# Tiles of x sums and mixer weights 64 bytes later, one product moved up, two splits and the first loads in another order

## The chip, the cores and the metric

The kernel runs on one core of one Trainium2 chip. The metric is the device time of one execution in microseconds. The profile gives names to the engines: PE (TensorE: matmuls; PEld is its weight load), DVE (VectorE), ACT (ScalarE), POOL (GpSimd) and SP (SyncE, which issues most of the DMAs).

## The reference

One decoder layer on x of 512 tokens by 1024 features, float32:

```python
x = x + 0.5 * rms_norm(swiglu_ffn(rms_norm(x, norm_pre[0]), ffn1_w_in, ffn1_w_out), norm_post[0])
mixed = token_mixer(rms_norm(x, norm_pre[1]), w_mix_in, conv_w, conv_b, gate_bias, lb, hg_norm, ml_norm, w_mix_out)
x = x + rms_norm(mixed, norm_post[1])
x = x + 0.5 * rms_norm(swiglu_ffn(rms_norm(x, norm_pre[2]), ffn2_w_in, ffn2_w_out), norm_post[2])

def swiglu_ffn(x, w_in, w_out):
    gate, up = jnp.split(x @ w_in, 2, axis=-1)      # 1024 -> 2 x 2816
    return (jax.nn.silu(gate) * up) @ w_out         # 2816 -> 1024
```

The token mixer projects h with one matrix, runs two chunked recurrences (HGRN2 and mLSTM, four heads each) and projects back.

## The kernel before

**Three products for one.** The big matmuls run in the type float32r. An operand is cast into a "hi" part by ACT, and DVE takes the rest (operand minus hi) into a "lo" part; both lie in one tile, hi first. A product is then hi·hi + hi·lo + lo·hi, three matmuls. For a weight tile this is a *split* (`split`, L195 the cast on ACT, L197 the subtraction on DVE, 128x1024 each). Behind its split an item may add one raw tile into another on POOL (L209), for the products that follow.

**The first matmul of an FFN** takes fewer products by block sums of x and of the weights. The 11 column pairs t = 0..10 each need seven products p1..p7 (pair 0 is done in parts named c1..c4 and e1..e4). One product is 24 matmuls of 128x128 by 128x256 (`prod`, L456): the stationary operand is a weight tile `w`, the moving one is a tile of x. The left operands: p1, p2, p4 and p5 read the tiles `xq`, p3, p6 and p7 read the tiles `sq`, which hold sums of x. So four of seven products of a pair move `xq`, three move `sq`. A constant list gives the order; for the first pairs it is written out, and from the fifth pair on a pair t has p1 of t, p4 of t-1, then p3, p5, p7, p6, p2 of t.

```python
ORDER = HEADS + [(p, 1) for p in ("p7", "p5", "p3", "p6")] + [("p5", 2), ("p7", 2), ("p3", 2), ("p4", 1), ("p6", 2)]
```

Pair index 2 is called the third pair here, index 3 the fourth. `feed` splits weights ahead in that order, into four `w` tiles; raw weights come in by DMA from SP. After a product `after` combines the PSUM banks on DVE and ACT (L475 to L489). After p6 these are n, q and the new half of the hidden tile (`hf<-q,ps`), in that order on DVE; the last one reads the bank of p7, into which p4 of the same pair accumulates. So p4 of a pair waits for the step behind p6 of that pair.

**Where the tiles lie.** The kernel's allocation before puts the four `xq` at byte 33440 + 8192 n of each partition, the four `w` at 87008 + 8192 n and the three tiles of the ring "s" at 179936 + 8192 n. The ring "s" holds first `sq` and then, in the second matmul of the FFN, the split hidden tiles `hs`. Modulo 128, `xq` begin at 32, `w` and the ring "s" at 96. Rows inside a tile are multiples of 512 bytes apart.

**The second matmul of an FFN** has `hs` stationary and `w` moving, 512 columns (`mm3`, L125 to L127). **The mixer** has jobs of two kinds: `in_k` (L409) with `w` stationary and `xq` moving, 256 columns, and `t_mm` (by `mm3`, L125 to L127) with `xq` stationary and `w` moving, 512 columns; the output projection is of the second kind. These have weight tiles of 2 by 512.

**The begin.** SP and ACT issue the loads of x by rows of 128 (i) and halves (h); the norm's gain row comes as one row and is spread over the partitions by PE (`gain_pe`, L114). `spin` issues matmuls of the identity whose result is not used (L121). Then rows 0 and 1 are normed (L329 to L348), turned by PE (L244) and split (L264, L266), and the product c1 begins.

**The head of the second FFN** (`ffn_head`) does the same for x of that stage while the output projection of the mixer ends. `behind(i)` makes what is traced in it come later on its engine than the instruction i. Outside the begin, a scheduler places each engine's instructions, by what it takes to be ready.

Of the kernel before, what the change touches and what calls it, by code (L numbers as in the profile page):

```python
# [19 lines left out]
ND = D // P  # L20
NF = FF // P
EPS = 1e-6
RAW, WBUF = 3, 4
PAIRS = NF // 2
HALF = T // 2
KH = ND // 2
# [13 lines left out]
HEAD = 3  # L40
HEADS = [("c1", 0), ("c3", 0), ("c2", 0), ("c4", 0), ("p1", 1), ("e1", 0), ("e3", 0)]
HEADS += [("e2", 0), ("p1", 2), ("p2", 1), ("e4", 0), ("p2", 2)]
ORDER = HEADS + [(p, 1) for p in ("p7", "p5", "p3", "p6")] + [("p5", 2), ("p7", 2), ("p3", 2), ("p4", 1), ("p6", 2)]
for _t in range(HEAD, PAIRS):
    if _t == HEAD:
        ORDER += [("p1", _t), ("p3", _t), ("p5", _t), ("p4", _t - 1)] + [(p, _t) for p in ("p7", "p6", "p2")]
    else:
        ORDER += [("p1", _t), ("p4", _t - 1)] + [(p, _t) for p in ("p3", "p5", "p7", "p6", "p2")]

# [9 lines left out]
class Item:  # L59

    def __init__(self, key, loads, rows=None, adds=(), dst=None):
        self.key, self.loads, self.rows, self.adds, self.dst = key, loads, rows, adds, dst
        self.reads = {key, *(k for pair in adds for k in pair)}


class Layer:
# [32 lines left out]
    def gain_pe(self, tag, row):  # L101

        nc = self.nc
        g = self.cp.tile([P, D], F32, tag=tag, bufs=1, name=self.nm(tag))
        r = self.hf[0:1, 14:16, :].rearrange("p a t -> p (a t)")
        nc.sync.dma_start(r, row)
        one = self.st("one", P)[:1]
        nc.gpsimd.memset(one, 1.0)
        self.spare = self.ps()
        self.spin(3)  # L110
        for h in range(2):
            ps = self.ps()
            v = slice(512 * h, 512 * h + 512)
            nc.tensor.matmul(ps, one, r[:, v], start=True, stop=True)  # L114
            nc.vector.tensor_copy(g[:, v], ps)
        return g
# [67 lines left out]
    def split(self):  # L184

        nc = self.nc
        it = self.items.popleft()
        raw = self.raw[it.key]
        _, a, b = raw.shape
        w = it.dst() if it.dst else self.wp.tile([P, 2, a, b], F32R, tag="w", bufs=WBUF, name=self.nm("w"))  # L190
        hi, lo = w[:, 0], w[:, 1]
        self.ready.append((w, it.dst is not None))
        rows = it.rows
        if rows is None:
            nc.scalar.copy(hi, raw)  # L195
            yield
            nc.vector.tensor_tensor(lo, raw, hi.bitcast(F32), op=ALU.subtract)  # L197
        else:
            for j in range(a):
                nc.scalar.activation(hi[:, j], raw[:, j], AF.Copy, scale=rows[:, j : j + 1])  # L200
            yield
            for j in range(a):
                nc.vector.scalar_tensor_tensor(
                    lo[:, j], raw[:, j], rows[:, j : j + 1], hi[:, j].bitcast(F32), op0=ALU.mult, op1=ALU.subtract
                )
        with self.behind(*self.hold):
            for out, other in it.adds:
                o, c = self.raw[out], self.raw[other]
                nc.gpsimd.tensor_tensor(o, o, c, op=ALU.add)  # L209
        self.load_due(self.done)  # L210
        self.done += 1
        yield

    def feed(self, most=WBUF):

# [55 lines left out]
    def sums(self, i, src):  # L271


        nc = self.nc
        v = slice((i % 2) * P, (i % 2 + 1) * P)
        f = [x[:, :, v] for x in self.xf]
        sub = lambda out, a, b: nc.vector.tensor_tensor(out, a, b, op=ALU.subtract)  # L277
        hi = lambda dst, src: nc.scalar.copy(dst[:, 0, :, v], src)
        lo = lambda dst, src: sub(dst[:, 1, :, v], src, dst[:, 0, :, v].bitcast(F32))
        p1, p0 = self.turn(src, 1), self.turn(src, 0)  # L280
        a22 = self.hf[:, 10 + i, :].rearrange("p (c t) -> p c t", c=KH)
        s1, s2, s3, s4 = self.xq[2], self.sq[2], self.sq[1], self.sq[0]
        hi(self.xq[2], p0)
        hi(self.xq[3], p1)
        nc.scalar.copy(a22, p1)
        lo(self.xq[2], p0)
        lo(self.xq[3], p1)
        yield
        sub(p1, p0, a22)
        sub(p0, f[0], p0)  # L290
        hi(s3, p0)
        lo(s3, p0)
        yield
        sub(p0, f[0], p1)
        hi(s1, p1)
        lo(s1, p1)
        yield
        hi(s2, p0)
        sub(p1, f[1], p0)
        lo(s2, p0)  # L300
        yield
        hi(s4, p1)
        lo(s4, p1)
        yield
# [127 lines left out]
    def open_ffn(self, ctx):  # L432

        hp = self.hpool = ctx.enter_context(self.tc.tile_pool(name=self.nm("hp"), bufs=1))
        self.hf = hp.tile([P, NF, T], F32, name=self.nm("hf"))
        self.xf = [self.hf[:, j : j + 2, :].rearrange("p a (b t) -> p (a b) t", t=HALF) for j in (NF - 4, NF - 2)]
        self.sq = [hp.tile([P, 2, KH, HALF], F32R, tag="s", bufs=3, name=self.nm("sq")) for _ in range(3)]
        self.left = {"p1": self.xq[0], "p2": self.xq[1], "p4": self.xq[3], "p5": self.xq[2], "p6": self.sq[2], "p7": self.sq[1], "p3": self.sq[0]}
        self.left.update({"c1": self.xq[0], "c2": self.xq[1], "c3": self.xq[0], "c4": self.xq[1]})
        self.left.update({"e1": self.xq[2], "e2": self.xq[3], "e3": self.xq[2], "e4": self.xq[3]})  # L440
        self.gs, self.held, self.copies = [], {}, []
        self.hs, self.bank, self.later, self.n, self.q, self.had = deque(), {}, deque(), {}, {}, set()
# [68 lines left out]
    def ffn_head(self, trans):  # L511

        norm, seen = self.normed, self.col()
        norm.append(self.nc.gpsimd.tensor_copy(seen, self.hf[:, 17, T - 1 :]))
        self.hold = norm[2:]
        self.full_split()
        with self.behind(*self.added):
            for _ in range(2):  # L520
                self.full_split()
        with self.behind(*norm):
            for g in self.copies:
                next(g)
            self.feed()
        S = lambda: [next(g) for g in self.gs]
        then = {("e1", 0): S, ("e3", 0): S, ("e2", 0): S, ("e4", 0): S}
        for n, (p, t) in enumerate(HEADS):
            self.feed()
            self.lag()  # L530
            self.prod(p, t)
            self.after(p, t)
            if n == 0:
                with self.behind(*norm):
                    trans(2)
            elif n == 2:
                trans(3)
            elif (p, t) in then:
                then[p, t]()
        self.hold = ()  # L540
        self.holes()

    def start(self, norm, xn):
# [2 lines left out]
        norm(1)  # L546
        q = [[self.part(i, h, xn[i]) for h in range(2)] for i in range(2)]
        step = lambda *gs: [next(g) for g in gs]
        self.spin(4)
        step(q[0][0], q[0][1], q[0][0])  # L550
        self.spin(4)
        split = self.split()
        step(q[1][0], q[1][1])
        next(split)
# [72 lines left out]

    def h_tile(self, k2, dst=None):

        t = dst if dst is not None else self.hpool.tile([P, 2, 2, T], F32R, tag="s", bufs=3, name=self.nm("hs"))  # L630
        src = self.hf[:, 2 * k2 : 2 * k2 + 2, :]
        self.nc.scalar.copy(t[:, 0], src)
        self.nc.vector.tensor_tensor(t[:, 1], src, t[:, 0].bitcast(F32), op=ALU.subtract)  # L633
        return t
# [106 lines left out]
    def mix_items(self):  # L741
# [2 lines left out]

        def item(src, a, b, rows=None):
            key = ("mix", len(made))
            made.append(Item(key, [Load(key, src, a, b)], rows))

        def f(c0):
            for n in range(4):  # L750
# [14 lines left out]
    def ffn_items(self, name, w_in, w_out):  # L765
# [26 lines left out]
        for p, t in ORDER:  # L792
            if p[0] == "e":
                continue
            dst = (lambda n=stay[p]: self.sq[n]) if p in stay else None
            made.append(Item((name, t, place[p]), own.get((p, t), ()), None, adds.get((p, t), ()), dst))
        for h in range(2):
            for k2 in range(PAIRS):
# [585 lines left out]
def layer(tc, aps):  # L1384
    with ExitStack() as ctx:
# [26 lines left out]
        with ExitStack() as f1:  # L1412
            L.open_ffn(f1)
            with tc.manual_schedule():
                first = L.start_loads()
                for i in range(NT):
                    for h in range(2):
                        v = slice(512 * h, 512 * h + 512)
                        (nc.scalar if i == 1 else nc.sync).dma_start(L.xs[:, i, v], x[0, i * P : (i + 1) * P, v])
                        if i == h == 0:  # L1420
                            gp[0] = L.gain_pe("gpre", pre[0:1, :])
                    if i:
                        L.load(first.popleft())
                    if i == 1:

                        nc.scalar.activation(L.col(), L.nhalf[:, :1], AF.Exp)
                while first:
                    L.load(first.popleft())
                L.start(norm, xn)
# [39 lines left out]
```

## Time and profile before

| | |
|---|---|
| time, median of 3 runs | 976.48 us (976.01 to 976.5) |
| the profiled execution: its time / its span | 976.29 us / 974.6 us |
| busy: PE / DVE / ACT / POOL | 960.6 / 695.0 / 464.0 / 291.5 us |
| granted clock of PE, mean | 0.997 |
| matmuls of `prod` that move `sq` / `xq` against `w` | 1440 / 2016 |
| splits (L195 and L197) | 214, besides 6 into the ring "s" |

Time outside the span is 1.7 us. A line of a view names the source line, the engine, the operation, and out<-in by tile names; a group's two numbers are busy time and mean duration. Matmuls overlap in the pipeline, so the duration of one is longer than the step from one start to the next. Rates below are therefore taken from start times: the start of one run of matmuls to the start of the next, divided by their number.

### The profile page before, as it was taken

The numbers are of one execution on the slowest core, as the hardware profiler recorded it, in microseconds if no ns is written. First come the engines' busy times: TensorE is split into PE (matmuls) and PEld (weight loads), VectorE is DVE, ScalarE is ACT, GpSimd is POOL, SyncE is SP. The second block draws the span as 40 slices with busy tenths as digits, with TensorE's granted clock in tenths as the row PEclk, the third lists the DMA queues.
The fourth block names the chain that finished last, engine by engine and source line by source line (L and its number), as shares of the span: only waits on it lengthen the run. The fifth ranks groups of instructions, "written<-read, shape, count | busy, mean of one in ns | idle before, by whom it ended". The sixth has DMA issues, their size and how long they took to land.

```text
span 974.6 us, 15937 instructions
## 1 busy us (share of the span) xinstructions
PE 960.6 (99%) x6595; PEld 884.9 (91%) x6595; DVE 695.0 (71%) x796; ACT 464.0 (48%) x625; POOL 291.5 (30%) x224
## 2 busy tenths in 40 slices
PE   8999999999999999999999999999999999999997
PEld 7999999999888889998887888899999999988885
DVE  5798888898545466697846564797988889854543
ACT  6644444445435356955622444564444444543531
POOL 3346555642000036200001210454565565200001
PEclk9999999999999999999999999999999999999999
DMA  9243334335322016321222126114332433233202
GB/s 317 74 130 109 109 90 129 109 109 151 108 100 95 1 25 172 90 85 44 66 65 66 44 82 214 37 58 130 108 110 88 128 110 108 88 109 101 94 1 87
DMA packets 81666, 95.98 MB, mean 98 GB/s; under 512 B 4117, under 2 KB 61497, under 8 KB 81594
## 3 DMA queue, kind: packets, MB, share of 16 engines
q1 hardware_dynamic: 81306, 94.44, 30.7%
q8 instruction: 52, 0.85, 0.4%
q10 hardware_dynamic: 288, 0.52, 0.2%
q14 instruction: 20, 0.16, 0.1%
HBM read 92.85 MB, written 2.10 MB: 97 GB/s over the span
## 4 chain that ended last, share of the span: by engine, by line
PE 91%; DVE 3%; issue 2%; POOL 2%; ACT 1%; DMA 1%; DVEq 0%; POOLq 0%; SPq 0%; ACTq 0%
PE ps L456 38%; PE ps L125 13%; PE ps L127 13%; PE ps L126 13%; PE ps L409 6%; PE ps L969 2%; POOL raw L209 2%; PE ps L419 1%; PE ps L244 1%; DVE w L197 1%; PE ps L1143 0%; ACT w L195 0%; DVE ps L277 0%; PE ps L114 0%; PE ps L1054 0%
## 5 line engine op out<-in xcount | busy, mean ns | idle before, releaser
L197 DVE TENSOR_TENSOR w<-raw,w 128x1024 fp32r<-128x1024 f32 x214 | 341.5, 1608 | 151.7 <-ACT w L195 151.0
L195 ACT CAST w<-raw 128x1024 fp32r<-128x1024 f32 x214 | 224.1, 1052 | 290.3 <-PE ps L127 116.5
L209 POOL TENSOR_TENSOR raw<-raw,raw 128x1024 f32<-128x1024 f32 x80 | 221.2, 2766 | 187.2 <-DVE w L197 170.2
L456 PE MATMUL ps<-xq,w 128*128 128x256 f32 x2016 | 239.9, 278 | 2.6 <-DVE hf L475 2.6
L456 PEld LDWEIGHTS ps<-xq,w 128*128 128x128 f32 x2016 | 235.3, 189 | 3.3 <-ACT w L195 2.3
L456 PE MATMUL ps<-sq,w 128*128 128x256 f32 x1440 | 178.9, 283 | 0.0
L456 PEld LDWEIGHTS ps<-sq,w 128*128 128x128 f32 x1440 | 174.9, 191 | 0.0
L127 PE MATMUL ps<-w,hs 128*128 128x512 f32 x336 | 131.0, 390 | 0.0
L125 PE MATMUL ps<-w,hs 128*128 128x512 f32 x336 | 130.9, 390 | 0.0
L126 PE MATMUL ps<-w,hs 128*128 128x512 f32 x336 | 130.8, 389 | 0.0
L125 PE MATMUL ps<-w,xq 128*128 128x512 f32 x208 | 84.8, 408 | 0.1
L126 PE MATMUL ps<-w,xq 128*128 128x512 f32 x208 | 81.6, 392 | 0.0
L127 PE MATMUL ps<-w,xq 128*128 128x512 f32 x208 | 81.5, 393 | 0.0
L127 PEld LDWEIGHTS ps<-w,hs 128*128 128x128 f32 x336 | 63.1, 188 | 13.6 <-DVE hs L633 0.7
L126 PEld LDWEIGHTS ps<-w,hs 128*128 128x128 f32 x336 | 63.1, 188 | 13.0
L125 PEld LDWEIGHTS ps<-w,hs 128*128 128x128 f32 x336 | 63.1, 188 | 12.9
L330 POOL TENSOR_SCALAR col<-col 128x1 f32<-128x1 f32 x24 | 9.7, 404 | 199.4 <-ACT junk L329 199.2
L409 PE MATMUL ps<-xq,w 128*128 128x256 f32 x480 | 56.5, 278 | 0.0
L409 PEld LDWEIGHTS ps<-xq,w 128*128 128x128 f32 x480 | 55.5, 188 | 0.0
L633 DVE TENSOR_TENSOR hs<-hf,hs 128x1024 fp32r<-128x1024 f32 x42 | 51.1, 1218 | 0.0
L125 PEld LDWEIGHTS ps<-w,xq 128*128 128x128 f32 x208 | 39.1, 188 | 9.0 <-ACT xq L250 0.8
L127 PEld LDWEIGHTS ps<-w,xq 128*128 128x128 f32 x208 | 39.0, 188 | 8.8 <-DVE xq L251 0.2
(230 smaller groups left out, 975.7 us busy)
## 6 DMA issues: line engine op xcount, KB each, us to landing
raw<-in_ffn_w_in_dram SPq DMA_DIRECT2D x88, 512.0 KB, 4.0
raw<-in_ffn_w_out_dram SPq DMA_DIRECT2D x44, 512.0 KB, 3.5
raw<-in_w_mix_in_dram SPq DMA_DIRECT2D x28, 512.0 KB, 3.8
raw<-in_w_mix_out_dram SPq DMA_DIRECT2D x8, 512.0 KB, 3.5
out_dram<-xs SPq DMA_DIRECT2D x8, 256.0 KB, 2.1
xs<-in_x_dram SPq DMA_DIRECT2D x6, 256.0 KB, 6.3
gpost<-in_norm_post_dram SPq DMA_DIRECT2D x3, 512.0 KB, 3.9
gpre<-in_norm_pre_dram SPq DMA_DIRECT2D x2, 512.0 KB, 4.2
```

Of the source, the lines that this page charges most:

```text
L125: mm(ps, sh, mh, start=start, stop=False, **kw)
L126: mm(ps, sh, ml, start=False, stop=False, **kw)
L127: mm(ps, sl, mh, start=False, stop=stop, **kw)
L195: nc.scalar.copy(hi, raw)
L197: nc.vector.tensor_tensor(lo, raw, hi.bitcast(F32), op=ALU.subtract)
L209: nc.gpsimd.tensor_tensor(o, o, c, op=ALU.add)
L244: self.nc.tensor.transpose(pt[:, c * P : (c + 1) * P], src[:, k * P : (k + 1) * P], self.ident)
L409: mm(ps[:, u0:u1], w[:, a, k, :], self.xop(k, b, u0, u1), start=k + n + m == 0, stop=k == ND - 1 and n == 2, skip_group_check=True,)
L419: self.nc.tensor.matmul(ps[:, :HALF], w[:, a, k, :], self.xop(k, b, 0, HALF), start=m + k == 0, stop=m == 2 and k == ND - 1)
L456: self.nc.tensor.matmul(ps[:, c], w[:, b, k, v], left[:, d, k, :], start=first and a + n + k == 0, stop=n == 2 and k == KH - 1, skip_group ...
L633: self.nc.vector.tensor_tensor(t[:, 1], src, t[:, 0].bitcast(F32), op=ALU.subtract)
L969: nc.tensor.matmul(sc[:, 64 * m : 64 * m + 64], k8[:, m], q8[:, m], start=True, stop=True)
```

## The change

1. **Places.** `w` tiles and the tiles of the ring "s" grow by 128 bytes (`PAD` = 32 floats). `sq`, and `w` tiles whose weights have the form 2 by 512 in the mixer, begin 64 bytes into the tile; everything else at its begin. So neighbours in a ring are 8320 bytes apart, and modulo 128 `sq` and the mixer's 2 by 512 weights begin at 32, all other weights and `hs` still at 96.
2. **Order.** p1 of the fourth pair now stands ahead of p6 of the third. The splits and the POOL adds tied to them move with the products, in both FFNs.
3. **Head of the second FFN.** Behind the norm two splits are traced instead of a full `feed`; in the first four products no `feed` stands ahead of the product (the one inside `pull` stays), and from the fifth on `feed` is traced behind the last lo part of `xq` (`self.lowed`).
4. **Begin.** The gain row is the first DMA on SP; the second half of rows 0 and 1 of x comes from ACT, the first half from SP (before: both of row 0 from SP, both of row 1 from ACT). `spin` runs 2, 3 and 2 instead of 3, 4 and 4 times.

```diff
-RAW, WBUF = 3, 4
+RAW, WBUF, PAD = 3, 4, 32
...
-ORDER = HEADS + ... + [("p5", 2), ("p7", 2), ("p3", 2), ("p4", 1), ("p6", 2)]
+ORDER = HEADS + ... + [("p5", 2), ("p7", 2), ("p3", 2), ("p4", 1), ("p1", 3), ("p6", 2)]
...
-        ORDER += [("p1", _t), ("p3", _t), ("p5", _t), ("p4", _t - 1)] + [(p, _t) for p in ("p7", "p6", "p2")]
+        ORDER += [("p3", _t), ("p5", _t), ("p4", _t - 1)] + [(p, _t) for p in ("p7", "p6", "p2")]
...
-        self.spin(3)
+        self.spin(2)
...
-        w = it.dst() if it.dst else self.wp.tile([P, 2, a, b], F32R, tag="w", bufs=WBUF, name=self.nm("w"))
+        if it.dst:
+            w = it.dst()
+        else:
+            w = self.place(self.wp.tile([P, 2 * D + PAD], F32R, tag="w", bufs=WBUF, name=self.nm("w")), a, it.late)
...
+    def place(self, t, a, late=False):
+        o = PAD // 2 if late else 0
+        return t[:, o : o + 2 * D].rearrange("p (b k t) -> p b k t", b=2, k=a)
...
-        lo(self.xq[3], p1)
+        self.lowed = lo(self.xq[3], p1)
...
-        self.sq = [hp.tile([P, 2, KH, HALF], F32R, tag="s", bufs=3, name=self.nm("sq")) for _ in range(3)]
+        sq = [hp.tile([P, 2 * D + PAD], F32R, tag="s", bufs=3, name=self.nm("sq")) for _ in range(3)]
+        self.sq = [self.place(t, KH, True) for t in sq]
+        self.stay = [self.place(t, KH) for t in sq]
...
-            self.feed()
+            for _ in range(2):
+                self.full_split()
...
-            self.feed()
+            if n > 3:
+                with self.behind(self.lowed):
+                    self.feed()
             self.lag()
             self.prod(p, t)
...
-        self.spin(4)
+        self.spin(3)
         step(q[0][0], q[0][1], q[0][0])
-        self.spin(4)
+        self.spin(2)
...
-            made.append(Item(key, [Load(key, src, a, b)], rows))
+            made.append(Item(key, [Load(key, src, a, b)], rows, late=b == 512))
...
-            dst = (lambda n=stay[p]: self.sq[n]) if p in stay else None
+            dst = (lambda n=stay[p]: self.stay[n]) if p in stay else None
...
+                gp[0] = L.gain_pe("gpre", pre[0:1, :])
                 for i in range(NT):
                     for h in range(2):
                         v = slice(512 * h, 512 * h + 512)
-                        (nc.scalar if i == 1 else nc.sync).dma_start(L.xs[:, i, v], x[0, i * P : (i + 1) * P, v])
-                        if i == h == 0:
-                            gp[0] = L.gain_pe("gpre", pre[0:1, :])
+                        (nc.scalar if i < 2 and h else nc.sync).dma_start(L.xs[:, i, v], x[0, i * P : (i + 1) * P, v])
```

The split hidden tiles of the second matmul are laid by `place` too, at the begin of their tile.

More of the change, by code (lines that the diff above doesn't have):

```diff
@@ L42 @@
 HEADS += [("e2", 0), ("p1", 2), ("p2", 1), ("e4", 0), ("p2", 2)]
-ORDER = HEADS + [(p, 1) for p in ("p7", "p5", "p3", "p6")] + [("p5", 2), ("p7", 2), ("p3", 2), ("p4", 1), ("p6", 2)]
+ORDER = HEADS + [(p, 1) for p in ("p7", "p5", "p3", "p6")] + [("p5", 2), ("p7", 2), ("p3", 2), ("p4", 1), ("p1", 3), ("p6", 2)]
 for _t in range(HEAD, PAIRS):
     if _t == HEAD:
-        ORDER += [("p1", _t), ("p3", _t), ("p5", _t), ("p4", _t - 1)] + [(p, _t) for p in ("p7", "p6", "p2")]
+        ORDER += [("p3", _t), ("p5", _t), ("p4", _t - 1)] + [(p, _t) for p in ("p7", "p6", "p2")]
     else:
@@ L59, with __init__ @@
 class Item:
-    def __init__(self, key, loads, rows=None, adds=(), dst=None):
-        self.key, self.loads, self.rows, self.adds, self.dst = key, loads, rows, adds, dst
+    def __init__(self, key, loads, rows=None, adds=(), dst=None, late=False):
+        self.key, self.loads, self.rows, self.adds, self.dst, self.late = key, loads, rows, adds, dst, late
         self.reads = {key, *(k for pair in adds for k in pair)}
@@ L628, in h_tile @@
     def h_tile(self, k2, dst=None):
-        t = dst if dst is not None else self.hpool.tile([P, 2, 2, T], F32R, tag="s", bufs=3, name=self.nm("hs"))
+        t = dst
+        if t is None:
+            t = self.place(self.hpool.tile([P, 2 * D + PAD], F32R, tag="s", bufs=3, name=self.nm("hs")), 2)
         src = self.hf[:, 2 * k2 : 2 * k2 + 2, :]
```

## The prediction

> **What bounds the kernel now.** I read the page's first part and its chain first, then the groups, and then runs of matmuls in the timeline, because a busy share of 99% says nothing of the rate.
>
> ```profile
> PE 960.6 (99%) x6595; PEld 884.9 (91%) x6595; DVE 695.0 (71%) x796; ACT 464.0 (48%) x625; POOL 291.5 (30%) x224
> PE 91%; DVE 3%; issue 2%; POOL 2%; ACT 1%; DMA 1%; DVEq 0%; POOLq 0%; SPq 0%; ACTq 0%
> L456 PE MATMUL ps<-xq,w 128*128 128x256 f32 x2016 | 239.9, 278 | 2.6 <-DVE hf L475 2.6
> L456 PE MATMUL ps<-sq,w 128*128 128x256 f32 x1440 | 178.9, 283 | 0.0
> ```
>
> PE bounds it, with DVE and POOL on the chain only in a few places. So there are two ways to be faster: a shorter step from matmul to matmul, and fewer waits of PE. The groups show that the same 128x256 matmul lasts 283 ns when `sq` moves and 278 when `xq` does. Starts show what that is in rate:
>
> ```profile
> 110.00 5.90 PE L456 MATMUL ps<-sq,w 128*128 128x256 f32 x48
> 115.75 8.34 PE L456 MATMUL ps<-xq,w 128*128 128x256 f32 x72
> 123.92 0.28 PE L456 MATMUL ps<-sq,w 128*128 128x256 f32 x1
> ```
>
> 48 matmuls that move `sq` take 115.75 - 110.00 = 5.75 us, 119.8 ns each; 72 that move `xq` take 8.17 us, 113.5 ns each. Nothing waits there. `sq` as the stationary operand (c1, c3, c4) is no slower, so the ring itself is not the cause. What differs is the place: `sq` and `w` both begin at 96 modulo 128, `xq` at 32.
>
> There is a second rate for the very same pair of tiles:
>
> ```profile
> 374.01 32.64 PE ps L409 x288
> 412.29 10.65 PE ps L409 x90
> ...
> 241.06 2.99 PE L456 MATMUL ps<-xq,w 128*128 128x256 f32 x24
> 243.89 0.39 PE L125 MATMUL ps<-w,hs 128*128 128x512 f32 x1
> ```
>
> With `xq` against `w`, 288 matmuls of the mixer take 113.3 ns each, and 90 others 118.3; p4 at 241.06 takes 2.83 us for 24, 117.9 each. I call these the fast and the slow step. The slow one begins behind other work or a wait and lasted through all 90. In the FFN it never lasts: three products later at most `sq` moves again, and the `xq` products behind that are at 113.5.
>
> The waits of PE and their surroundings:
>
> ```profile
> 69.64 3.07 PE L456 MATMUL ps<-xq,w 128*128 128x256 f32 x24 [0.49 <-DVE hf L475]
> 72.55 0.64 PE L456 MATMUL ps<-sq,w 128*128 128x256 f32 x4
> ...
> 86.06 4.43 PE L456 MATMUL ps<-xq,w 128*128 128x256 f32 x24 [2.14 <-DVE hf L475]
> ...
> 644.63 2.54 PE L456 MATMUL ps<-xq,sq 128*128 128x256 f32 x20 [1.32 <-DVE xq L277]
> ...
> 710.72 134.28 PE ps L456 x1152
> 86.00:90.00 4.00, 3.94 (x23) 3.97 (x24) 4.00 (x5) 0.25 (x1) 0.55 (x1) 0.66 0.91 282
> ```
>
> The two at 69.64 and 86.06 are p4 of the second and third pair in the first FFN, waiting for the step behind p6 of their pair. After the second, the granted clock is 0.66 for 4 us: 23 matmuls in a time for 34 at 118 ns, 1.3 us lost. The product at 710.72 (p4 of the fourth pair, second FFN) begins a new piece of the chain.
>
> **Term 1: `sq` 64 bytes later.** Then `sq` stands to `w` as `xq` does. 60 products of 24 matmuls move `sq`; at the fast step throughout, this is 1440 x 6.3 ns = 9.1 us. But the change also takes away what ended the slow step: no product with the old relation is left. A pair now costs 24 x (4 x 113.5 + 3 x 119.8) = 19.52 us. All fast it is 24 x 7 x 113.5 = 19.07 (-0.45), all at 118 it is 19.82 (+0.30).
>
> In the first FFN, 52 products (7.4 pairs) follow p4 of the third pair: -3.3 us fast, +2.2 us slow. The 7 `sq` products before it gain 1.1 us, which I count at nothing, since the p4 at 69.64 waits for DVE and would only wait longer. In the second FFN 9 `sq` products come before 710.72 (-1.4 us), and 48 products from there on: -3.1 fast, +2.1 slow. The p4 products behind waits (69.64: 2.91 us to the next product; 241.06) all ran slow, so I expect at least one FFN to fall into the slow step at a p4 and stay. With one slow and one fast, the term is +2.2 - 1.4 - 3.1 = -2.3 or -3.3 - 1.4 + 2.1 = -2.6: I take -2.4. Both fast is -7.8, both slow +2.9.
>
> The Trainium skill, page "TensorE: Matmul & The Clock Gate", Part 2, speaks against this term: moving operand and weight load have two independent read ports of SBUF, so that loading weights takes nothing from the running matmul. By that the places of tiles would not matter and this term and the next would be zero; the 119.8 against 113.5 ns speak against it.
>
> **Term 2: the mixer's 2 by 512 weights.**
>
> ```profile
> 445.41 0.39 PE L125 MATMUL ps<-w,xq 128*128 128x512 f32 x1
> 447.47 0.39 PE L125 MATMUL ps<-w,xq 128*128 128x512 f32 x1
> ...
> 299.65 0.39 PE L125 MATMUL ps<-w,hs 128*128 128x512 f32 x1
> 301.46 0.39 PE L127 MATMUL ps<-w,hs 128*128 128x512 f32 x1
> ```
>
> Nine matmuls between the first two starts, 2.06 us: 228.9 ns each, with `w` at 96 and `xq` at 32. Eight between the other two, 1.81 us: 226.3 ns, both at 96. For 512 columns equal places are the better ones. The change makes `w` and `xq` equal: 576 matmuls (four jobs of 96, and 192 in the output projection) x 2.6 ns = 1.5 us at most. Some of this lies where PE waits for the recurrences; I take -1.0. `hs` and the FFN's `w` keep their relation: nothing.
>
> **Term 3: p1 of the fourth pair ahead of p6 of the third.**
>
> ```profile
> 71.31 2.40 POOL L209 TENSOR_TENSOR raw<-raw,raw 128x1024 f32<-128x1024 f32 x1 [5.95 <-DVE w L197]
> 74.87 5.79 POOL L209 TENSOR_TENSOR raw<-raw,raw 128x1024 f32<-128x1024 f32 x2 [1.16 <-DVE w L197]
> ...
> 75.85 0.69 DVE L475 TENSOR_TENSOR ps<-ps,n 128x512 f32<-128x512 f32 x1
> 79.30 2.44 DVE L197 TENSOR_TENSOR w<-raw,w 128x1024 fp32r<-128x1024 f32 x1 [2.77 <-ACT w L195]
> 81.67 0.68 DVE L475 TENSOR_TENSOR n<-ps,hf 128x512 f32<-128x512 f32 x1
> ...
> 85.23 0.68 DVE L475 TENSOR_TENSOR hf<-q,ps 128x512 f32<-128x512 f32 x1
> ```
>
> DVE stands 2.77 us before the split of p5 of the fourth pair, whose raw tile is the POOL add at 74.87, the add tied to p1. Behind that split stand n, q and the new half of p6, though p6 ended on PE at 72.55 + 2.87 = 75.4. With p1 first, its add takes the place at 71.31 and the split of p5 can go at some 76 us, three earlier. Against that, p6 runs one product (2.8 us) later and p4 comes two products behind it instead of three. From p6's new end, 78.2, n, q, the half and a split of p4 between them need 3 x 0.7 + 1.2 to 3.0 (a split beside a POOL add), and the split of p5 may reach to 79.4: the half is ready between 82.5 and 84.7. p4 is due at 83.9. So a wait of up to 0.8 us is left of 2.14, and the half clock (1.3) goes: 1.3 to 3.4 us won, I take -2.6. In the second FFN this place has no wait to remove.
>
> The Trainium skill, same page, Part 1, has the clock fall to half after an idle window of some 3.4 us. The 2.14 us here were enough for 0.66, so the row decides; by the rule the term would be 1.3 us smaller.
>
> **Term 4: the begin.**
>
> ```profile
> 0.79 0.39 SPq L1419 DMA_DIRECT2D xs<-in_x_dram  x1
> 1.24 0.32 SPq L106 DMA_DIRECT2D hf<-in_norm_pre_dram  x1
> ...
> 8.92 1.41 DVE L348 SCALAR_TENSOR_TENSOR xn<-xs,col,gpre 128x512 f32<-128x512 f32 x2
> 10.79 1.42 DVE L348 SCALAR_TENSOR_TENSOR hf<-xs,col,gpre 128x512 f32<-128x512 f32 x2 [0.45 <-POOL col L334]
> ...
> 8.21 2.08 PE L121 MATMUL ps<-ident 128*128 128x128 f32 x8
> 10.07 1.91 PE L244 MATMUL ps<-ident,xn 128*128 128x128 f32 x8
> 11.78 1.27 PE L121 MATMUL ps<-ident 128*128 128x128 f32 x8
> 12.89 1.04 PE L244 MATMUL ps<-ident,hf 128*128 128x128 f32 x8
> 14.16 1.08 PE L456 MATMUL ps<-xq,sq 128*128 128x256 f32 x7 [0.24 <-ACT xq L264]
> ```
>
> The gain row is issued 0.45 us earlier, so L114 and the norm of row 0 come 0.45 earlier; row 1 loses its 0.45 wait for POOL at best, as the squares of row 0 get their second half sooner. The fewer turns of `spin` give way for that: they hold PE until 10.07 and 12.89. So c1 begins 0.45 to 1.2 us earlier. On the other side, up to 11.78 a matmul takes (11.78 - 10.07) / 8 = 214 ns, half clock; with PE less busy the clock could rise later, and 24 matmuls of c1 at 214 instead of 113 would cost 2.4 us. I take -0.7, nearest to the first bound.
>
> **Term 5: head of the second FFN.**
>
> ```profile
> 633.29 1.42 DVE L348 SCALAR_TENSOR_TENSOR hf<-xs,col,gpre 128x512 f32<-128x512 f32 x2 [0.80 <-POOL col L334]
> 635.76 5.70 DVE L197 TENSOR_TENSOR w<-raw,w 128x1024 fp32r<-128x1024 f32 x3
> 641.38 1.28 DVE L277 TENSOR_TENSOR xq<-ps,xq 128x512 fp32r<-128x512 f32 x2
> 643.89 1.28 DVE L277 TENSOR_TENSOR xq<-ps,xq 128x512 fp32r<-128x512 f32 x2
> ```
>
> Three splits stand ahead of the lo parts of `xq`, for whose second pair PE waits 1.32 us. Two of the three lose their place behind the norm. If they fall behind the lo parts or into gaps, the 1.32 goes; if the scheduler puts them into the norm of row 3, that chain is up to 2 x 1.2 us later. I take -0.4, half of the gap of 0.80.
>
> **The sum.** Profiled time 976.3 (span 974.6 and 1.7 around it; the median of the runs is 0.2 higher): 976.3 - 2.4 - 1.0 - 2.6 - 0.7 - 0.4 = 969.2.
>
> **The rivals.**
> - *Both FFNs fast.* For it: every slow stretch seen began at a wait or behind other work, and the waits are few. Against: p4 at 69.64 waits still. 976.3 - 7.8 - 4.7 = 963.8.
> - *Both slow.* For it: the three p4 above; one short wait anywhere is enough. Against: `c` and `e` products behind waits came out fast (644.63 and what follows). 976.3 + 2.9 - 4.7 = 974.5.
> - *Places do nothing* (the change doesn't do what it says): the 119.8 would belong to `sq` for another reason. Terms 1 and 2 fall out: 972.6. Against: the second pair of places, in the mixer, differs too. The rule of the two ports, told above from the Trainium skill, would lead here.
> - *Slower: the shorter way from p6 to p4.* If the step behind p6 is not held by POOL but by the mass of splits ahead of it on DVE, its lag stays: 85.9 - 75.4 = 10.5 us behind p6's end, now 78.2 + 10.5 = 88.7. p4 of the third pair then begins 2.8 us later than now, and the half clock lasts 1.5 us longer: +4.3 instead of -2.6; as the wait also starts the slow step in both FFNs, 976.3 + 2.9 + 4.3 - 1.0 - 0.7 - 0.4 = 981.4. It decides as soon as the half `hf<-q,ps` ends more than 7.7 us behind p6.
>
> **How the numbers follow.** One slow, one fast 0.37; both fast 0.15; both slow 0.25; places do nothing 0.11; slower 0.12. About 0.2% (2 us) is what a measurement of this kernel can tell from no change. Below 974.5: the first two, most of the fourth, and nearly half of the third (its terms 3 to 5 are uncertain by some 2 us): 0.72. Within: the other part of the third, mainly: 0.14. Above 978.4: 0.14. The range leaves out half of the fastest case and the slower rival: 963 to 977.5.
>
> **What would show it.** Right: runs of 24 with `sq` at 113 to 114 ns, or whole FFNs at 118 with no change at `sq`; 226 to 227 ns in the mixer's 512-column runs; no half clock near 86 us; c1 before 13.8 us; a shorter wait in e1. Wrong: `sq` still at 119.8 while `xq` is at 113.5; p4 of the third pair waiting over 2 us; half clock inside c1; steps that change from one `w` buffer to the next, since neighbours are now 8320 bytes apart, which no run of before shows.

## The result, and the profile after

The changed kernel takes 982.68 us (median, 981.82 to 984.13) against 976.49 for the kernel before: the ratio is 1.0064, with a 95% interval of 1.0047 to 1.0082. It is slower by 6.2 us, where 7 us less were forecast. The profiled execution took 984.13 us, with a span of 982.4.

The page of the changed kernel; in the group rows the first number behind the bar is the busy time in us, the second the mean of one in ns:

```profile
PE 967.1 (98%) x6587; PEld 887.3 (90%) x6587; DVE 703.7 (72%) x796; ACT 464.4 (47%) x625; POOL 289.2 (29%) x224
PE 87%; DVE 8%; issue 2%; ACT 1%; POOL 1%; DMA 1%; POOLq 0%; DVEq 0%; ACTq 0%
L466 PE MATMUL ps<-xq,w 128*128 128x256 f32 x2016 | 245.8, 281 | 5.3 <-DVE hf L485 5.3
L466 PE MATMUL ps<-sq,w 128*128 128x256 f32 x1440 | 175.0, 280 | 0.0
L125 PE MATMUL ps<-w,hs 128*128 128x512 f32 x336 | 132.1, 393 | 0.0
L127 PE MATMUL ps<-w,hs 128*128 128x512 f32 x336 | 132.0, 393 | 0.0
L126 PE MATMUL ps<-w,hs 128*128 128x512 f32 x336 | 131.9, 393 | 0.0
L125 PE MATMUL ps<-w,xq 128*128 128x512 f32 x208 | 85.1, 409 | 0.1
L126 PE MATMUL ps<-w,xq 128*128 128x512 f32 x208 | 81.6, 393 | 0.0
L127 PE MATMUL ps<-w,xq 128*128 128x512 f32 x208 | 81.6, 393 | 0.0
```

The rows of the second FFN matmul and of the mixer in the page of before, which the prediction did not show:

```profile
L127 PE MATMUL ps<-w,hs 128*128 128x512 f32 x336 | 131.0, 390 | 0.0
L125 PE MATMUL ps<-w,hs 128*128 128x512 f32 x336 | 130.9, 390 | 0.0
L126 PE MATMUL ps<-w,hs 128*128 128x512 f32 x336 | 130.8, 389 | 0.0
...
L125 PE MATMUL ps<-w,xq 128*128 128x512 f32 x208 | 84.8, 408 | 0.1
L126 PE MATMUL ps<-w,xq 128*128 128x512 f32 x208 | 81.6, 392 | 0.0
L127 PE MATMUL ps<-w,xq 128*128 128x512 f32 x208 | 81.5, 393 | 0.0
```

PE is busy 6.5 us longer with the same products. The products that move `sq` did get shorter (178.9 to 175.0 us), but those that move `xq` got longer by more (239.9 to 245.8), and so did the second FFN matmul, which the prediction left out: 392.7 to 396.0. The chain gives PE 87% instead of 91 and VectorE 8% instead of 3. The timeline of PE in the changed kernel shows where (start and length in us):

```profile
2.99 3.78 PE L114 MATMUL ps<-hf,one 1*128 1x512 f32 x4 [0.22 <-DMA hf<-in_norm_pre_dram]
...
8.21 1.97 PE L252 MATMUL ps<-ident,xn 128*128 128x128 f32 x8
...
12.04 2.21 PE L466 MATMUL ps<-xq,sq 128*128 128x256 f32 x17 [0.24 <-ACT xq L272]
...
73.55 5.82 PE L466 MATMUL ps<-sq,w 128*128 128x256 f32 x48
79.21 2.99 PE L466 MATMUL ps<-xq,w 128*128 128x256 f32 x24
86.65 5.46 PE L466 MATMUL ps<-xq,w 128*128 128x256 f32 x24 [4.45 <-DVE hf L485]
...
125.93 2.88 PE L466 MATMUL ps<-sq,w 128*128 128x256 f32 x24
128.65 2.88 PE L466 MATMUL ps<-xq,w 128*128 128x256 f32 x24
131.37 5.82 PE L466 MATMUL ps<-sq,w 128*128 128x256 f32 x48
137.03 8.64 PE L466 MATMUL ps<-xq,w 128*128 128x256 f32 x72
145.51 0.73 PE L466 MATMUL ps<-sq,w 128*128 128x256 f32 x5
...
649.08 4.98 PE L466 MATMUL ps<-xq,sq 128*128 128x256 f32 x40 [0.96 <-DVE xq L285]
```

Three things are to be seen. c1 begins at 12.04 instead of 14.16. p4 of the third pair, at 86.65, waits 4.45 us where it waited 2.14, and then takes 5.3 us for 24 matmuls. And from 125.93 on the step changes with no wait between: 24 of `sq` in 2.72 us (113.3 ns), 24 of `xq` at 113.3, then 48 of `sq` in 5.66 us (117.9) and 72 of `xq` in 8.48 (117.8). Both are signs that the prediction named against itself: a wait of over 2 us at that p4, and a rate that changes from one product to the next.

The changed kernel's allocation says why the second was to be feared. Its four `w` lie at 87008 + 8320 n, which is 224, 96, 224 and 96 modulo 256, and `xq` at 160 as before. So modulo 256 `xq` lies 64 bytes below two of the `w` tiles and 64 above the other two, where before it lay 64 below all four.

The clock around that p4 (columns as in the prediction; the last but two is the granted clock), and VectorE's queue ahead of it:

```profile
86.60:93.00 6.40, 6.35 (x31) 6.38 (x32) 5.87 (x5) 0.85 (x1) 2.37 (x1) 0.53 0.36 110
```

```profile
77.05 2.83 DVE L200 TENSOR_TENSOR w<-raw,w 128x1024 fp32r<-128x1024 f32 x1
79.80 0.68 DVE L485 TENSOR_TENSOR hf<-ps,hf 128x512 f32<-128x512 f32 x1
80.40 3.04 DVE L200 TENSOR_TENSOR w<-raw,w 128x1024 fp32r<-128x1024 f32 x1
83.37 0.68 DVE L485 TENSOR_TENSOR n<-ps,hf 128x512 f32<-128x512 f32 x1
...
85.82 0.68 DVE L485 TENSOR_TENSOR hf<-q,ps 128x512 f32<-128x512 f32 x1
```

p6 of the third pair ends on PE at 76.4 (half of the 48 at 73.55). The step behind it (n, q and the new half `hf<-q,ps`, on VectorE; not the step from matmul to matmul) begins at 83.37, behind two splits of 2.83 and 3.04 us, and ends at 86.50, 10.1 us behind p6. VectorE is never idle here, but the step stands last.

### The profile page after: what moved, and what is told of

It reads as the page before. It is cut to its first block, busy times and chain, and to the rows that moved or that the text cites. A ratio compares the mean times of both kernels' runs of the same rounds, so it can differ in the third digit from the quotient of the medians.

```text
span 982.4 us, 15914 instructions
## 1 busy us (share of the span) xinstructions
PE 967.1 (98%) x6587; PEld 887.3 (90%) x6587; DVE 703.7 (72%) x796; ACT 464.4 (47%) x625; POOL 289.2 (29%) x224
## 4 chain that ended last, share of the span: by engine, by line
PE 87%; DVE 8%; issue 2%; ACT 1%; POOL 1%; DMA 1%; POOLq 0%; DVEq 0%; ACTq 0%
PE ps L466 37%; PE ps L125 12%; PE ps L127 12%; PE ps L126 12%; PE ps L417 6%; DVE w L200 4%; PE ps L984 2%; PE ps L252 1%; DVE hf L485 1%; ACT junk L337 1%; POOL col L338 0%; PE ps L1158 0%; PE ps L114 0%; PE ps L1069 0%; PE ps L1265 0%
## 5 line engine op out<-in xcount | busy, mean ns | idle before, releaser
L200 DVE TENSOR_TENSOR w<-raw,w 128x1024 fp32r<-128x1024 f32 x214 | 351.0, 1650 | 151.7 <-ACT w L198 151.3
L466 PE MATMUL ps<-xq,w 128*128 128x256 f32 x2016 | 245.8, 281 | 5.3 <-DVE hf L485 5.3
L466 PEld LDWEIGHTS ps<-xq,w 128*128 128x128 f32 x2016 | 240.9, 190 | 6.2 <-issue 6.0
L466 PE MATMUL ps<-sq,w 128*128 128x256 f32 x1440 | 175.0, 280 | 0.0
L466 PEld LDWEIGHTS ps<-sq,w 128*128 128x128 f32 x1440 | 171.5, 188 | 0.0
L417 PE MATMUL ps<-xq,w 128*128 128x256 f32 x480 | 56.7, 279 | 0.0
L417 PEld LDWEIGHTS ps<-xq,w 128*128 128x128 f32 x480 | 55.7, 188 | 0.0
```

Source lines behind the costliest of these rows:

```text
L417: mm(ps[:, u0:u1], w[:, a, k, :], self.xop(k, b, u0, u1), start=k + n + m == 0, stop=k == ND - 1 and n == 2, skip_group_check=True,)
L466: self.nc.tensor.matmul(ps[:, c], w[:, b, k, v], left[:, d, k, :], start=first and a + n + k == 0, stop=n == 2 and k == KH - 1, skip_group ...
```

## The experiments

All were timed in turn with the kernel before on the same chip, whose median was 976.9 to 977.3 each time.

**Each part alone.** *places_only* has the placing of the tiles and nothing else of the change, *order_only* the two lines of `ORDER`, *begin_only* the row, its loads and the turns of `spin`, *head_only* the two splits and `lowed`.

> The kernel before with only the places changed (w and the s ring 8320 bytes apart instead of 8192, x sums and the mixer's 2 by 512 weights 64 bytes later). Theory 'neighbour distance': the new distance costs about 3.4 us in the two output matmuls of the FFNs (1008 matmuls of 512 columns at 230.8 instead of 227.4 ns) and mixes 113 and 118 ns steps product by product in the FFN inputs, so the time is 979 to 982. Rival 'the order is to blame for the whole loss': the places gain about what was forecast (terms 1 and 2, -3.4), so about 973.

> The kernel before with only p1 of the fourth pair ahead of p6 of the third. Theory 'the lag behind p6 stays': p4 of the third pair begins 0.5 to 2.8 us later than before and waits 4 to 5 us in place of 2.14, with a longer half clock: 977.5 to 980. Rival 'the wait grew only because the products around it ran faster or slower in the new places': the forecast of -1.3 to -3.4 holds here, 973 to 975.

> The kernel before with only the earlier norm row, its loads and the fewer turns of TensorE. Theory 'the begin shifts everything': c1 begins 2.1 us earlier as in the changed kernel, and 1.3 to 2.1 us of it reach the end: 974.4 to 975.2. Rival 'the wait at p4 of the third pair, which hangs on VectorE and GpSimd, takes it back': 976 to 977.

> The kernel before with only the two splits behind the cast in the head of the second FFN. Theory 'the order on VectorE hardly changes': the wait of e1 shrinks by 0.3 to 0.4 us, 976.1. Rival 'a split that comes later starves a product': 977 or more.

| | us | against before | ratio, 95% |
|---|---|---|---|
| places_only | 980.85 | +3.86 | 1.0033 to 1.0058 |
| order_only | 980.27 | +3.28 | 1.0024 to 1.0049 |
| begin_only | 975.13 | -1.86 | 0.9972 to 0.9989 |
| head_only | 976.96 | 0.0 | 0.9992 to 1.0010 |

places_only and begin_only came as their theories said, order_only 0.3 us above the range of its theory, and head_only shows no change, which neither of its two had. The four sum up to +5.3 of the 6.2; the 0.9 between is within what the intervals leave open. In places_only the row `w,hs` is that of the changed kernel (396.0 us in all), `xq,w` is 3.9 longer and `sq,w` 3.7 shorter than before: the gain at `sq` is paid back at `xq`, and the loss at `w,hs` is left. In order_only p4 begins at 88.25 and waits 4.39 us. The loss thus has two causes, which the next runs take one by one.

**Which part of the places?** *w_8320* leaves every tile at the begin of its buffer and only makes the `w` buffers longer:

```
-w = it.dst() if it.dst else self.wp.tile([P, 2, a, b], F32R, tag="w", ...)
...
+    w = self.wp.tile([P, 2 * D + 32], F32R, tag="w", ...)
+    w = w[:, o : o + 2 * D].rearrange("p (b k t) -> p b k t", b=2, k=a)      # o is 0
```

> The kernel before with only the w buffers 8320 bytes apart instead of 8192; nothing is laid later, sq and hs keep their ring. Theory 'neighbour distance': w,hs goes from 226.8 to 230 or 231 ns (1008 matmuls, +3.4 us) and xq,w products run partly at 118 (half of 72 products x 24 x 4.5 ns = +3.9 at most): 979 to 983, with sq still at 119.8. Rival 'the loss in the changed kernel comes from the shifted sums': w,hs and xq,w as before, 976 to 977.5.

983.76 us, ratio 1.0069 (1.0057 to 1.0081). With nothing laid later, the groups give 396.0 us for `w,hs` (+3.3), 242.8 for `xq,w` (+2.9) and 177.9 for `sq,w` (-1.0). The distance of 8320 alone costs as much as the whole change; in places_only, where the sums move too, the loss is 3 us smaller.

Matching the matmuls in order with the places of the allocation shows the two relations side by side. Of the 1008 `w,hs` matmuls, half have `w` in the same place as `hs` modulo 256 and step at 227.4 ns on average; the other half lie 128 bytes apart and step at 233.0, where before all 1008 were equal at 226.8. Of the 60 products that move `sq`, 31 have `w` 128 bytes away and step at 118.4 ns; the 29 with equal places step at 119 to 120 (one at 123.6), as before. Modulo 128 these two kinds don't differ, so already here the places count modulo 256.

*sq_64* and *sq_192* keep the distance at 8192. The `s` ring becomes one tile with three slots, and the sums begin 64 or 192 bytes into a slot, the split weights of the c products and `hs` at its begin:

```
+self.ring, self.nh = hp.tile([P, 6 * D + 48], F32R, ...), 0   # sq_64: 6 * D + 16
+slot = (0, 2, 1)
+self.sq = [self.view(slot[n], 48, KH) for n in range(3)]   # sq_64: 16
+self.stay = [self.view(slot[n], 0, KH) for n in range(3)]
```

> The kernel before with only the x sums 64 bytes later: the s ring is one tile, so its slots stay 8192 bytes apart, and w and hs keep their places. Theory 'only the places modulo 128 count, and it was the new neighbour distance that mixed the steps': products that move sq go from 119.8 to 113.4 or 118 ns per matmul and keep that rate over many products; w,hs stays at 226.8; time 969 to 974.5, as term 1 forecast (-2.4, at most -7.8). Rival 'places count modulo 256 too': xq is 64 bytes below w and sq 64 above it (modulo 256), the rate changes between 113 and 118 at every change from xq to sq, and the time is 975 to 977.

> As sq_64, but the sums lie 192 bytes later, so that modulo 128 nothing differs from sq_64, and modulo 256 sq stands to w exactly as xq does. If only modulo 128 counts: the same as sq_64 within 0.7 us. If modulo 256 counts: one rate for whole FFNs, 968.7 with both at 113.4, 972 to 974 with one at 118, and faster than sq_64 by 2 us or more.

sq_64: 976.82 us, ratio 0.9997. sq_192: 976.93 us, but with single runs from 969.22 to 981.37. First sq_64, then sq_192 (`sr` is `sq` here):

```profile
123.48 2.99 PE L463 MATMUL ps<-sr,w 128*128 128x256 f32 x24
126.31 2.89 PE L463 MATMUL ps<-xq,w 128*128 128x256 f32 x24
129.04 5.82 PE L463 MATMUL ps<-sr,w 128*128 128x256 f32 x48
134.69 1.53 PE L463 MATMUL ps<-xq,w 128*128 128x256 f32 x12
```

```profile
87.42 3.06 PE L463 MATMUL ps<-xq,w 128*128 128x256 f32 x24 [2.54 <-DVE hf L482]
90.32 5.82 PE L463 MATMUL ps<-sr,w 128*128 128x256 f32 x48
95.97 5.82 PE L463 MATMUL ps<-xq,w 128*128 128x256 f32 x48
102.87 2.97 PE L463 MATMUL ps<-xq,w 128*128 128x256 f32 x24 [1.08 <-DVE hf L482]
105.67 2.88 PE L463 MATMUL ps<-sr,w 128*128 128x256 f32 x24
108.39 2.88 PE L463 MATMUL ps<-xq,w 128*128 128x256 f32 x24
```

In sq_64 `sq` takes 117.9 ns (24 from 123.48 to 126.31) and 117.7 (48 from 129.04 to 134.69), `xq` 113.7 between. In sq_192 both have one rate: 117.7 from the wait at 87.42 to the next wait, 113.3 behind that one. By the medians alone nothing would be decided: sq_192 is not 2 us faster than sq_64, as the second theory had it, but the same. The rates decide, and the spread of the runs (12 us against 3.6). Only 128 bytes differ between the two kernels, so places count at least modulo 256, not only modulo 128. And sq_192 is what term 1 described, whole stretches at one rate, chosen at a wait: its runs span 969.2 to 981.4, where the prediction's "both fast" and "both slow" for this term alone are 968.5 and 979.2 (976.3 - 7.8, + 2.9). The wait that chooses the rate can be short. In the second FFN of sq_192 the slow rate that lasts to the FFN's end begins with the product at 784.26, where two starts are 231 and 194 ns apart in the place of 113; the timeline lists no wait there.

The Trainium skill, page "TensorE: Matmul & The Clock Gate", Part 2, has weight load and moving operand on two independent read ports, so that loading weights takes nothing from the running matmul. By that the step would not hang on how the two tiles lie to each other; between sq_64 and sq_192 only a place in memory differs, and the rate of `sq` with it. The measurement decides: the step does hang on it here. No run shows the ports themselves.

*after_8448* repairs the changed kernel with two numbers, 8448 being 33 times 256:

```
-RAW, WBUF, PAD = 3, 4, 32
+RAW, WBUF, PAD = 3, 4, 64
-o = PAD // 2 if late else 0
+o = 48 if late else 0
```

> The changed kernel with two numbers other: w and s buffers 8448 bytes apart (33 times 256) instead of 8320, and the late ones 192 bytes later instead of 64. Theory 'the distance of 8320 is all that was wrong with the places': w,hs back at 226.8 ns (-3.4 us), no change of rate from one w buffer to the next, sq at 113.4 or 118 for whole stretches; with the loss by the order (+3.3) and the gain at the begin (-1.9) single runs lie between 970 and 981, the median under the changed kernel's 982.7. The mixer's 512-column matmuls with w and xq then differ by 128 bytes modulo 256: 226.5 if only modulo 128 counts, 229 or more if not. Rival 'any growth of the buffers costs': 981 to 984 and w,hs at 230.

976.89 us, runs from 974.55 to 980.87, ratio 1.0001 (0.9988 to 1.0014): no difference from the kernel before, where the changed one is 6.2 above it. `w,hs` is back at 392.7 us, and the mixer's `w,xq` at 247.1 where before has 247.9 and the changed kernel 248.3. One sentence of the expectation was wrong: `w` laid 192 bytes later begins at 160 modulo 256, and so does `xq`, so the mixer's matmuls have equal places, not places 128 bytes apart, and the run can't tell modulo 128 from modulo 256 for them. The longer buffer cost `w,hs` nothing here, as its length keeps the places modulo 256.

*p6_equal* tests what ends the slow rate. It lays only the sums of p3 and p7 192 bytes later, so that p6 still moves a tile with the same place as `w`:

```
+slot = (1, 2, 0)
+self.sq = [self.view(slot[n], (48, 48, 0)[n], KH) for n in range(3)]
```

> The kernel before with the sums of p3 and p7 192 bytes later, as in sq_192, and those of p6 in their old place, equal to w. Theory 'a product with equal places ends the slow rate, and places 64 bytes apart modulo 256 run at whichever rate was there before': p6 stays at 119.8, p3 and p7 go to 113.4, a slow rate after a wait lasts only to the next p6; 2 x 24 x 6.4 ns = 0.31 us a pair, 971.5 to 973.5, and the times of single runs lie within 2 us, not 12 as in sq_192. Rival 'the slow rate comes by chance at any product': single runs as far apart as in sq_192, median 975 to 977.

972.39 us, ratio 0.9949 (0.9937 to 0.9962), runs from 970.16 to 974.51: the median is in the range of the theory, the spread of 4.4 us is over its 2 but far from the 12 of sq_192. Behind a wait of p4 in its timeline:

```profile
102.48 3.06 PE L463 MATMUL ps<-xq,w 128*128 128x256 f32 x24 [1.24 <-DVE hf L482]
105.38 2.99 PE L463 MATMUL ps<-sr,w 128*128 128x256 f32 x24
108.21 2.99 PE L463 MATMUL ps<-xq,w 128*128 128x256 f32 x24
111.03 5.86 PE L463 MATMUL ps<-sr,w 128*128 128x256 f32 x48
116.73 8.34 PE L463 MATMUL ps<-xq,w 128*128 128x256 f32 x72
124.91 1.30 PE L463 MATMUL ps<-sr,w 128*128 128x256 f32 x10
```

p3 and p5 take 2.83 and 2.82 us (117.7 ns), p7 and p6 5.70 together; the three products behind p6 take 8.18 us, 113.6 each. A product with equal places costs 6.5 ns a matmul itself (119.8 against 113.3) and brings the fast rate back: so it is behind 19 of the 20 p6 of this trace, and behind the other one PE stalls within the next product (one start comes after 188 ns). Not all of the 4.9 us need be the rate's: in the profiled run the wait of p4 of the third pair (2.38 us) was followed by a granted clock of 1.00, not 0.66 as before. How much that is over all runs is not known.

**Why was p6's step late?** *begin_p2* goes the other way than the change: on the changed begin, p2 of the fourth pair stands ahead of p4 of the third, one product more between.

```
-ORDER += [("p1", _t), ("p3", _t), ("p5", _t), ("p4", _t - 1)] + [(p, _t) for p in ("p7", "p6", "p2")]
+ORDER += [(p, _t) for p in ("p1", "p3", "p5", "p2")] + [("p4", _t - 1), ("p7", _t), ("p6", _t)]
```

> The kernel with only the begin changed, and in it p2 of the fourth pair ahead of p4 of the third (p1, p3, p5, p2, then p4, p7, p6). Theory 'p4 needs a product more behind p6, not one less': the 2.2 us wait of p4 goes, p2 may wait up to 1.6 us for its weights instead, and no half clock follows: 971.5 to 974. Rival 'VectorE is full in this stretch, the wait only changes its place': 975 to 976.5.

981.62 us, outside both ranges. p4 of the third pair no longer waits, but behind p6 of the fourth there is now no p2, and that pair's p4 waits 5.42 us. The step behind p6 is no faster; with four products of 2.8 us behind that p6 it is covered, and the pair that gave the fourth product pays. The rival was right that the wait only changes its place, and had the price too low.

*step_first* keeps the order before and queues the splits behind p6 of the third pair behind its step:

```
+self.step = tt(h1, self.two_by(q), self.two_by(bank["p7", t]), ALU.subtract)
...
+if was == ("p6", HEAD - 1):
+    with self.behind(self.step):
+        self.feed()
+else:
+    self.feed(WBUF - 1 if (p, t) == ("p6", HEAD - 1) else WBUF)
```

> The kernel before, in its own order of products, but the splits of p5 and p4 behind p6 of the third pair are put behind the step of that p6 (n, q, new half) on VectorE. Theory 'p6's step is late because it stands behind splits that wait for GpSimd': n, q and hf go into the 2.8 us in which VectorE was idle, p4 of the third pair waits under 0.6 us instead of 2.14 and no half clock follows (2.4 + 1.3 us): 973 to 974.5. Rival 'the stretch is short of VectorE time as a whole': p5 or p4 waits for its split instead, 976 to 978.

979.96 us, ratio 1.0024 (1.0015 to 1.0032), above both ranges. VectorE stood still over 4.07 us, for the Silu of the pair before, and this Silu stood on ScalarE behind a cast that waited for GpSimd's add; p5 then waited for its split on PE. ScalarE, and PE:

```profile
79.49 1.05 ACT L195 CAST w<-raw 128x1024 fp32r<-128x1024 f32 x1 [8.01 <-POOL raw L209]
...
81.85 0.58 ACT L489 ACTIVATE ps<-ps 128x512 f32<-128x512 f32 x1
```

```profile
82.28 2.00 PE L456 MATMUL ps<-xq,w 128*128 128x256 f32 x16
86.26 0.95 PE L456 MATMUL ps<-xq,w 128*128 128x256 f32 x6 [1.98 <-DVE w L197]
```

*step_silu* queues those casts behind that Silu as well (`with self.behind(self.step, self.silu)`). *order_step* is step_first on the changed order.

> step_first, and the casts of the splits that come later also queued behind the Silu of the second pair's p4 on ScalarE. Theory 'in step_first the chain only changed its queue: the Silu, and with it q and hf, stood behind a cast that waits for GpSimd': the 4 us idle time of VectorE goes, hf ends by 81, the splits of p5 and p4 end by 82.9 and 85, PE waits under 1 us in all there: 973 to 975.5. Rival 'too much VectorE work': 977 to 980 as step_first.

> The order of order_only (p1 of the fourth pair ahead of p6 of the third), with the step behind that p6 queued on VectorE ahead of the split of p4. Theory 'the lag is the place of p6's step behind the splits of p5 and p4': hf ends some 6 us behind p6 instead of 10, p4 of the third pair begins within 0.6 us of being due and waits at most 1.5 us for its own split later; no long half clock: 975 to 977.5, 3 us or more under order_only. Rival 'VectorE has too much work there whatever its order': 979 to 981.

step_silu: 976.02 us (0.9983 to 1.0000), 3.9 under step_first. order_step: 978.12 us, 2.2 under order_only. Both lie between the ranges of the two theories. First p4 of the third pair in order_only, then order_step:

```profile
88.25 3.96 PE L456 MATMUL ps<-xq,w 128*128 128x256 f32 x17 [4.39 <-DVE hf L475]
```

```profile
84.75 2.98 PE L456 MATMUL ps<-xq,w 128*128 128x256 f32 x24 [0.24 <-DVE hf L475]
...
101.33 0.90 PE L456 MATMUL ps<-xq,w 128*128 128x256 f32 x3 [2.40 <-DVE hf L475]
```

The wait of 4.39 us at p4 of the third pair is 0.24, though VectorE does the same work: it was the place in the queue. But PE, now earlier, meets the same wait one pair later (2.40 us there, 1.81 in step_silu). So the gain was there and was given back.

**Put together.** *joined* has the changed begin, p6_equal and step_first; *begin_p6_equal* the first two; *joined_silu* has step_silu in the place of step_first; *joined_two* does the same for p6 of the fourth pair.

> The changed begin, step_first and p6_equal in one kernel, everything else as before. If the three add up (-1.9, -3, -4.5): 966.5 to 968.5. If an earlier PE in the first FFN only waits longer for VectorE: 970 to 973.

> The changed begin and p6_equal, order and splits as before. If they add up: 970.5 (972.4 - 1.9). If the earlier begin is lost in the wait of p4: 972 to 973.

> The changed begin, p6_equal and step_silu in one kernel. If step_silu is worth 2 to 3.5 us and adds up: 967 to 969. If not: as joined, 970 to 971.5.

> joined_silu, with the same queueing (step of p6 ahead of the next splits, casts behind the Silu) for the p6 of the fourth pair too, whose p4 waits 2.2 us there and runs at half clock after it. If the wait again only hangs on the place in the queues: 964.5 to 966.5. If the split that now comes later (of a product due at about 93) takes it over: 967 to 970.

| | us | ratio, 95% |
|---|---|---|
| joined | 970.76 | 0.9925 to 0.9949 |
| begin_p6_equal | 970.14 | 0.9917 to 0.9942 |
| joined_silu | 968.19 | 0.9899 to 0.9924 |
| joined_two | 963.81 | 0.9851 to 0.9883 |

begin_p6_equal adds up (970.5 was expected). joined is no better, so step_first is worth nothing there either; joined_silu is 2 us better, as step_silu gave to expect. joined_two is below its better range, and 13.2 us under the kernel before: the wait that was left had the same cause. PE waits at neither p4 in it (the second product of the row at 78.77, the third of the row at 89.79):

```profile
78.77 5.60 PE L463 MATMUL ps<-xq,w 128*128 128x256 f32 x48
...
89.79 8.34 PE L463 MATMUL ps<-xq,w 128*128 128x256 f32 x72
```

## Why the prediction was wrong

- **Term 1, `sq` 64 bytes later (-2.4): wrong.** The fast and the slow step, and a rate that is kept from wait to wait, are right, as sq_192 shows. Two steps of the argument failed. "`sq` stands to `w` as `xq` does" was worked out modulo 128, and the rates differ modulo 256 (sq_64 against sq_192). And the distance of 8320 was named as a danger in the last paragraph, but had no term in the sum: it puts neighbours 128 bytes apart modulo 256, so the rate changes from product to product, and `xq` loses what `sq` wins. In places_only that is +3.9 and -3.7 us, +0.2 in the place of -2.4.
- **"`hs` and the FFN's `w` keep their relation: nothing": wrong,** +3.3 us (392.7 to 396.0), most of the 3.9 that places_only loses. They keep it modulo 128 only; modulo 256 a little over half of these matmuls have their tiles 128 bytes apart. after_8448 takes the loss away.
- **Term 2, the mixer (-1.0): wrong by the same distance.** +0.4 in the changed kernel; -0.8 in after_8448, close to the term. By the places, half of the 576 matmuls got equal places in the changed kernel (median step 227 ns where before has 229), and the other half places 128 bytes apart (232).
- **Term 3, the order (-2.6): wrong; the slower rival was right in mechanism.** order_only costs 3.3, the rival said 4.3. What failed is "n, q, the half and a split of p4 between them" from p6's end: n stood behind that split and the one of p5, 2.8 and 3.0 us beside the adds, one more split stood ahead of hf, and hf ended 10.1 us behind p6, over the 7.7 from which the rival was to decide. The add tied to p1 did move ahead; the place in VectorE's queue held hf. order_step, where the queue differs and not the work, takes the wait from 4.39 to 0.24.
- **Term 4, the begin (-0.7): right in sign, too small.** The term was taken near the earlier issue, 0.45 us. The row was waited for less by far: the matmul that spreads it began at 2.99 instead of 4.50, the transposes of row 0 at 8.21 instead of 10.07, c1 2.1 us earlier; begin_only is worth 1.9. No half clock came into c1 (granted 1.00 from 12.04 to 20).
- **Term 5, the head (-0.4): nothing,** as the doubt in it allowed. head_only waits 1.33 us in e1, as before, and ends at the same time. The 0.96 in the changed kernel is therefore not the head's alone; what else made it shorter was not tried.
- **The weights.** The slower rival got 0.12 beside 0.52 for the cases with a fast FFN. Term 3 rested on one end of a sum whose queue the trace showed to be longer. That the rival's 981.4 lies so near the measured 982.7 is in part luck: its +4.3 for the order is the mechanism that came (+3.3), but its +2.9 stood for two FFNs at the slow step throughout, and the 3.9 that the places cost came from the distance of 8320, which no case had.

## What to carry to other kernels

A buffer that grows moves all its neighbours: work out how the two operands of every kind of matmul lie to each other before and after (here modulo 256), for the matmuls that the edit doesn't mean to touch too. A step that is late by its place in an engine's in-order queue isn't helped by having its trigger moved; follow the queue ahead of it on every engine that feeds it, and expect PE to meet the same wait one stage on until each stage has it mended. Measure the parts of a joined change alone: here a gain of 1.9 us lay hidden under two losses.

## What the runs showed of the hardware that was not expected

- The step of a 128x256 matmul behind matmuls of its kind was 113.3, 117.8, 118.4 or 119.8 ns by how its two tiles lie modulo 256 and by what ran before: 119.8 for equal places, 118.4 for places 128 bytes apart (w_8320), 117.8 for `sq` 64 bytes above `w` beside `xq` 64 below it (sq_64). With all tiles 64 below `w` (sq_192) it was 113.3 or 117.8, kept until a wait.
- In the changed kernel the relation alone doesn't set the rate. Of its products counted whole, those 64 below `w` ran 35 times near 113 and 39 near 118, those 64 above 10 and 62; the `xq` product at 128.65 is one of the ten. What chooses there is open, and why the chip does any of this no run shows.
- The step of a 128x512 matmul of the second FFN was about 227 ns for equal places modulo 256 and 233 for places 128 bytes apart (w_8320).
- The half clock doesn't follow the length of the wait alone. 2.14 us before, 2.40 in order_step and 4.45 in the changed kernel were followed by a granted clock of 0.66, 0.60 and 0.53, while 2.54 us in sq_192 left it at 1.00. Nearly the same wait did both: 2.34 us in sq_64 were followed by 0.61, and 2.38 in p6_equal by 1.00.

```profile
87.40:90.40 3.00, 2.98 (x25) 3.00 (x26) 3.00 (x4) 0.21 (x1) 0.00 (x0) 1.00 0.92 285
```

The Trainium skill, page "TensorE: Matmul & The Clock Gate", Part 1, has the clock fall after at least one idle window of some 3.4 us, and has that window run freely. That the same wait halves the clock or not agrees with the free running; that 2.14 us were enough does not agree with a whole idle window. No run here shows the window itself.
